# The first stage of a diffusion block in another order: x first on its queue, one-column token sums, projection from the first channels

## The chip, the core and the metric

One NeuronCore of a Trainium2 chip runs the whole program; the other seven are unused. The time is the device time of one execution in microseconds (us). Five engines work beside each other and meet only at semaphores: TensorE (PE; its weight loads have a row of their own, PEld), VectorE (DVE), ScalarE (ACT), GpSimd (POOL) and SyncE (SP), which here only issues transfers. Each engine takes its instructions in the order in which they stand on it.

## The reference

One layer of a transformer-like block on 512 tokens of 1024 channels, with 256 context tokens. What matters here is how it begins:

```
c_act = silu(c);  cc_act = silu(c_ctx)
shift, scale = parts of (c_act @ w_mod + b_mod)        # one value per channel
h = rmsnorm(x, norm1_g) * (1 + scale) + shift          # rmsnorm: x * rsqrt(mean over channels of x*x + eps) * g
proj = h @ w_in                                        # pooling, Fourier, Hyena, attention, gates
# Hyena's filters: two sine layers, a linear layer, a decay, a spectrum
f = sin(freq * (feats @ w1 + b1));  f = sin(freq * (f @ w2 + b2));  f = (f @ w3 + b3) * (decay + 0.05)
f = f / sum |f|
```

Behind that come the four branches, their gated merge, the output projection, a second norm, a gated feed-forward network with 2816 hidden channels and a last norm.

## The kernel before, in words

Channels lie on the partitions, in eight tiles of 128; the 512 tokens lie along the free dimension. A product in nearly full float32 precision is made of three passes: each operand is split into a high part (rounded to the type fp32r) and a low rest, and `mm3` (line 99) adds high x high, high x low and low x high. ACT makes the high part of a weight tile (tile `winh`), DVE the low one (`winl`); the same is done to the normalized x (`hxh`, `hxl`).

The change is in the first stage, lines 211 to 491. Between lines 387 and 491 the flag `pinned` is set, so that each engine's instructions keep exactly the order in which the calls stand there; behind it a scheduler orders the work. The stage has four threads:

- Statistics of x. `square(k)` (line 267) squares channel tile k on ACT, and PE multiplies the square by a matrix of ones (tile `pss`), which sums over the channels. `stat_sums` copies one row and turns it so that tokens lie on the partitions (`pst`). `rms_cols` (line 142) makes 1/sqrt on DVE and ACT from it, `rms_rows` (line 157) spreads that over the partitions with four diagonal matrices `dg` (PE, tile `pb`), and ACT copies it to `rb`.
- Modulation. `load_mod(kt)` loads 1 MB of weights (`wm`, four buffers), `mod(kt)` (line 348) multiplies them by c (PE, tile `pmod`; ACT copies it to `mrow`), and `mod_cols(kt)` (line 356) turns `mrow` to channels on the partitions (PE, tile `pmodt`; three small DVE operations `modk`, `acol`).
- The norm of tile kt: `norm` (DVE `hm`, ACT `hxh`) and `norm_low` (DVE `hxl`); then `estep(kt)` (line 382) adds this channel tile to three output tiles of the input projection (tile `pin`, three passes each).
- Hyena's filters: `sine_in`, `sine_arg`, `sine_out` for two layers (PE `pf`, ACT `san`, DVE `san`, ACT `h`), `fw3_fold` (DVE), `filt(s)` for four quarters of the taps (PE `ph`, DVE `khat`, ACT `vx`), `filt_abs`, and `fold(0..5)` (PE `pKe`, `pKo`).

Before, the threads are interleaved by twos: `mod` of two tiles, other PE work, then `mod_cols` of both, then the norm of both, and `estep` later. All loads stand on SP: first five small tables, then x, then weights.

Of the kernel before, what the change touches and what calls it, by code (L numbers as in the profile page):

```python
# [8 lines left out]
F32 = mybir.dt.float32  # L9
# [37 lines left out]
def block_kernel(ctx: ExitStack, tc: tile.TileContext, A):  # L47
# [3 lines left out]
    # an engine whose instructions keep the program's order while pinned is set  # L51
# [104 lines left out]
    # the same, spread over the partitions (tokens on the free dimension)  # L156
# [9 lines left out]
    # the table of the square root, loaded ahead of its use  # L166
# [18 lines left out]
    with ExitStack() as mix:  # L185
# [22 lines left out]
        # =================== start: modulation, first norm, filters of hyena ===================  # L208
# [6 lines left out]
        with ExitStack() as st:  # L215
# [19 lines left out]
            # filters of hyena: the two sine layers  # L235
            sines = (("h1", fw1, feats, h1), ("h2", fw2, h1, h2[0:64]))
            sans = []

            def sine_in(layer):
                _, w, src, _ = sines[layer]  # L240
                sans.append(yslot("san", (64, 4, TC), F32))
                for h, c in enumerate(halves):
                    p = ps("pf")[0:64, :TC]
                    PE.matmul(p, w, src[:, c], start=True, stop=True)
                    S.activation(sans[layer][:, h], p, AF.Identity, bias=frb[:, layer:layer + 1], scale=fr[:, 0:1])

            def sine_arg(layer):
                an = [(sans[layer][:, h], sans[layer][:, 2 + h]) for h in range(2)]
                for a, n in an:
                    V.tensor_scalar(n, a, INV2PI, MAGIC, ALU.mult, ALU.add)  # L250
                for a, n in an:
                    V.tensor_scalar(n, n, -MAGIC, None, ALU.add)
                for c in (C1, C2, C3):
                    for a, n in an:
                        V.scalar_tensor_tensor(a, n, -c, a, ALU.mult, ALU.add)
                for a, n in an:
                    V.tensor_scalar(a, a, PI_LO, -PI_LO, ALU.min, ALU.max)

            def sine_out(layer):
                dst = sines[layer][3]  # L260
                for h, c in enumerate(halves):
                    S.activation(dst[:, c], sans[layer][:, h], AF.Sin)
# [25 lines left out]
            # the sum of both directions' magnitudes is the larger magnitude of their sum and difference  # L288
# [24 lines left out]
            # transform at the odd frequencies f < 128; from sums over t = 4 u + r for each r follow those of  # L313
            # f, 511 - f, 255 - f and 256 + f (the second and third with the sine part negated)
            def fold(j):
# [11 lines left out]
                else:  # L327
                    # tabK's last part is that of t mod 4 = 3 negated
# [12 lines left out]
            # shift and scale of the first norm, channel tile by channel tile, for c and c_ctx  # L341
# [40 lines left out]
            def estep(kt):  # L382
                for m in range(NE):
# [4 lines left out]
            preload_sqrt(ones[:, 0:1])  # L388
            Y.dma_start(cols, A["cols"])
            V.tensor_scalar(frb, fr[:, 1:3], fr[:, 0:1], None, ALU.mult)  # L390
            Y.dma_start(feats, A["feats"])
            Y.dma_start(fw1, A["fw1"])
            Y.dma_start(fw2, A["fw2"])
            Y.dma_start(cc, A["cc"])
# [6 lines left out]
            Y.dma_start(sel, A["sel"])  # L401
            sine_arg(0)
            Y.dma_start(ident, A["ident"])
            load_mod(0)
            square(2)
            load_early()
            square(3)
            sine_out(0)
            fw3_fold()
            square(4)  # L410
            square(5)
            S.activation(cc, cc, AF.Silu)
            sine_in(1)
            load_mod(1)
            sine_arg(1)
            square(6)
            square(7)
            split_early()
            sums = stat_sums()
            rcx = rms_cols(sums)  # L420
            Y.dma_start(dec, A["dec"])
            load_mod(2)
            sine_out(1)
            mod(0)
            mod(1)
            load_mod(3)
            S.copy(rbx, rms_rows(rcx))
            mod_cols(0)
            mod_cols(1)
            norm(0)  # L430
            norm(1)
            filt(0)
            filt(1)
            norm_low(0)
            filt_abs(0)
            load_early()
            norm_low(1)
            split_early()
            load_early()
            mod(2)  # L440
            load_mod(4)
            split_early()
            load_mod(5)
            mod(3)
            filt(2)
            estep(0)
            estep(1)
            filt_abs(1)
            mod_cols(2)
            Y.dma_start(tabK, A["tabK"])  # L450
            mod_cols(3)
            norm(2)
            mod(4)
            mod(5)
            load_mod(6)
            norm(3)
            norm_low(2)
            fold(0)
            load_mod(7)
            fold_sum(0)  # L460
            filt(3)
            mod_cols(4)
            mod_cols(5)
            norm(4)
            norm_low(3)
            norm(5)
            mod(6)
            norm_low(4)
            fold(1)
            estep(2)  # L470
            estep(3)
            mod_cols(6)
            mod(7)
            norm(6)
            norm_low(5)
            fold_sum(1)
            norm_low(6)
            estep(4)
            mod_cols(7)
            norm(7)  # L480
            estep(5)
            filt_abs(2)
            fold(2)
            estep(6)
            norm_low(7)
# [3 lines left out]
            filt_abs(3)  # L489
# [27 lines left out]
        # =================== input projection, hyena ===================  # L517
# [694 lines left out]
```

## Time and profile before

| | us |
|---|---|
| median of 3 runs (range) | 866.44 (866.24 to 866.78) |
| span of the profiled execution | 864.0 |
| the median run, less that span | 2.4 |
| PE busy in the span | 843.5 (98%) |
| DVE, ACT, POOL busy | 501.2, 333.1, 6.0 |
| start of the first `pmod` in the stage | 20.83 |
| end of the stage's last filter product (`pKe`) | 68.47 |

The profile gives no time of its own for the profiled execution beyond its span; what lies around the span is taken to be the 2.4 us by which the median run is longer. A busy PE is not a PE at its peak, since matmuls overlap; so the table is no proof of a bound, and the rows below are.

### The profile page before, as it was taken

The page shows a single profiled execution, that of the slowest core. Times are in us where ns is not written, and L with a number is a line of the kernel's source. Part 1 is how long each engine was busy: PE and PEld are TensorE (multiplying, and loading weights), DVE is VectorE, ACT ScalarE, POOL GpSimd, SP SyncE. Part 2 cuts the span into 40 slices and gives each one's busy share as a digit, 9 for nine tenths or more (in the row PEclk, how much of TensorE's full clock was granted, in tenths as well). Part 3 has the DMA queues.
Part 4 walks back from the last instruction along what each step waited for, and adds up shares of the span by engine and source line. Part 5 has one row for each costly group of instructions (what it writes and reads, how often), then busy time and mean ns, then how long its engine had stood idle before and what let it go on. Part 6 is the DMA issues. An engine that isn't in the chain of part 4 may idle for free.

```text
span 864.0 us, 10732 instructions
## 1 busy us (share of the span) xinstructions
PE 843.5 (98%) x4192; PEld 685.5 (79%) x4192; DVE 501.2 (58%) x870; ACT 333.1 (39%) x519; POOL 6.0 (1%) x16
## 2 busy tenths in 40 slices
PE   6999999989999999999999999999999999999996
PEld 2577889777777778888888998888888888888886
DVE  4879997698797773444444774444444444233233
ACT  7544452625453342323333363333333333232321
POOL 0100000000000000000000000000000000000000
PEclk9999999999999999999999999999999999999998
DMA  8912214545555532223332222222222223223222
GB/s 315 414 50 74 98 43 162 164 168 180 195 183 183 199 137 92 91 92 116 124 126 98 73 89 108 98 98 98 98 98 98 98 94 95 86 92 91 86 68 98
DMA packets 30362, 107.30 MB, mean 124 GB/s; under 512 B 3783, under 2 KB 4935, under 8 KB 29288
## 3 DMA queue, kind: packets, MB, share of 16 engines
q1 hardware_dynamic: 30312, 106.62, 35.2%
q8 instruction: 33, 0.54, 0.2%
q14 instruction: 17, 0.14, 0.0%
HBM read 104.51 MB, written 2.10 MB: 123 GB/s over the span
## 4 chain that ended last, share of the span: by engine, by line
PE 86%; DVE 8%; ACT 2%; DMA 2%; issue 1%; SPq 0%; DVEq 0%; ACTq 0%
PE pup L60 28%; PE pin L60 25%; PE pdn L60 14%; PE pwo L60 5%; PE pbr L60 5%; PE psc L60 1%; DVE za L60 1%; PE pav L60 1%; PE pKe L60 1%; PE psl L60 1%; DVE winl L60 1%; DVE zb L60 1%; PE ptl L60 1%; DMA cb<-in_crow_dram 1%; PE pmod L60 1%
## 5 line engine op out<-in xcount | busy, mean ns | idle before, releaser
L60 PE MATMUL pup<-hxh,wupl 128*128 128x512 f32 (+1 forms) x376 | 140.8, 376 | 0.0
L60 PE MATMUL pup<-hxl,wuph 128*128 128x512 f32 (+1 forms) x376 | 140.6, 376 | 0.0
L60 PE MATMUL pup<-hxh,wuph 128*128 128x512 f32 (+1 forms) x376 | 139.9, 376 | 0.7 <-ACT wuph L60 0.4
L60 PE MATMUL pdn<-act,wdnh 128*128 128x512 f32 (+1 forms) x396 | 112.7, 368 | 0.0
L60 PE MATMUL pin<-hxh,wgh 128*128 128x512 f32 x256 | 101.4, 396 | 0.6 <-ACT wgh L60 0.6
L60 PE MATMUL pin<-hxh,wgl 128*128 128x512 f32 x256 | 100.5, 393 | 0.0
L60 PE MATMUL pin<-hxl,wgh 128*128 128x512 f32 x256 | 100.3, 392 | 0.0
L60 DVE TENSOR_TENSOR wupl<-wupr,wuph 128x1024 fp32r<-128x1024 f32 x44 | 53.9, 1225 | 71.5 <-ACT wuph L60 69.7
L60 ACT CAST wuph<-wupr 128x1024 fp32r<-128x1024 f32 x44 | 46.3, 1053 | 92.3 <-PE pup L60 86.3
L60 PEld LDWEIGHTS pdn<-act,wdnh 128*128 128x128 f32 x396 | 71.6, 189 | 12.0
L60 PEld LDWEIGHTS pup<-hxh,wuph 128*128 128x128 f32 x376 | 70.1, 188 | 13.8 <-ACT wuph L60 0.6
L60 PEld LDWEIGHTS pup<-hxh,wupl 128*128 128x128 f32 x376 | 70.7, 188 | 12.9 <-DVE wupl L60 0.2
L60 PEld LDWEIGHTS pup<-hxl,wuph 128*128 128x128 f32 x376 | 70.6, 188 | 12.9
L60 PE MATMUL pdn<-act,wdnl 128*128 128x512 f32 (+1 forms) x198 | 72.4, 366 | 0.0
L60 ACT ACTIVATE sg<-pin 128x512 f32<-128x512 f32 x32 | 19.2, 600 | 119.5 <-PE pin L60 119.5
L60 DVE TENSOR_TENSOR wdnl<-wdnr,wdnh 128x1024 fp32r<-128x1024 f32 (+1 forms) x24 | 27.2, 1134 | 63.2 <-ACT wdnh L60 63.1
L60 DVE SCALAR_TENSOR_TENSOR sg<-sg,pbr 128x512 f32<-128x512 f32 x24 | 16.5, 688 | 80.2 <-PE pbr L60 80.2
L60 PEld LDWEIGHTS pin<-hxh,wgh 128*128 128x128 f32 x256 | 48.1, 188 | 10.8 <-ACT wgh L60 1.0
L60 PEld LDWEIGHTS pin<-hxh,wgl 128*128 128x128 f32 x256 | 48.1, 188 | 10.5 <-issue 0.5
L60 PEld LDWEIGHTS pin<-hxl,wgh 128*128 128x128 f32 x256 | 48.1, 188 | 10.1 <-issue 0.5
L60 PE MATMUL pin<-hxh,winh 128*128 128x512 f32 x128 | 51.7, 404 | 0.0
L60 ACT CAST wdnh<-wdnr 128x1024 fp32r<-128x1024 f32 (+1 forms) x24 | 23.6, 982 | 72.4 <-PE pdn L60 66.7
(265 smaller groups left out, 1429.2 us busy)
## 6 DMA issues: line engine op xcount, KB each, us to landing
wupr<-in_wup_dram SPq DMA_DIRECT2D x44, 512.0 KB, 3.4
wgr<-in_wg_dram SPq DMA_DIRECT2D x32, 640.0 KB, 3.8
wm<-in_wmB_dram SPq DMA_DIRECT2D x32, 512.0 KB, 4.7
wm<-in_wmA_dram SPq DMA_DIRECT2D x8, 1024.0 KB, 10.7
winr<-in_win_dram SPq DMA_DIRECT2D x16, 512.0 KB, 3.5
wdnr<-in_wdn_dram SPq DMA_DIRECT2D x16, 512.0 KB, 3.4
wor<-in_wout_dram SPq DMA_DIRECT2D x8, 512.0 KB, 3.5
wdnr<-in_wdn_dram SPq DMA_DIRECT2D x8, 384.0 KB, 3.0
```

Source lines behind the costliest of these rows:

```text
L60: ins = f(*a, **k)
```

## The change

The order of the stage's calls is new, and some pieces are computed in another way:

- SP loads x first; the five small tables (`cols`, `feats`, `fw1`, `fw2`, `cc`) are issued by ACT. `ident` and `sel` follow x, and the weights follow in another order.
- `square` runs on DVE for tiles 0, 1, 2 and 7, on ACT for 3 to 6. Four products with a single column of ones, the square as the stationary operand, put the sums on the token partitions at once; `stat_sums` is gone.
- The tables of Silu and of the square root are loaded ahead of the statistics, the sine's table once, behind them.
- The sine layers' two token halves stand on 64 partitions each, so that `sine_arg` has 6 operations instead of 12. `fw3_fold` runs on POOL.
- Each channel tile goes through `mod`, `mod_cols`, `norm`, `norm_low` by itself, and the projection's `estep` of the tile before stands between them.

```diff
             def sine_in(layer):
                 _, w, src, _ = sines[layer]
-                sans.append(yslot("san", (64, 4, TC), F32))
-                for h, c in enumerate(halves):
+                sans.append(yslot("san", (P, 2, TC), F32))
+                for r, c in zip(rows, halves):
...
             def sine_arg(layer):
-                an = [(sans[layer][:, h], sans[layer][:, 2 + h]) for h in range(2)]
-                for a, n in an:
-                    V.tensor_scalar(n, a, INV2PI, MAGIC, ALU.mult, ALU.add)
...
+                a, n = sans[layer][:, 0], sans[layer][:, 1]
+                V.tensor_scalar(n, a, INV2PI, MAGIC, ALU.mult, ALU.add)
...
             def square(k):
                 sq = tmp(T)
-                S.activation(sq, xs[k], AF.Square)
-                PE.matmul(pss, ones, sq, start=k == 0, stop=k == KT - 1)
-
-            def stat_sums():
-                S.copy(ssq[0:1], pss[0:1])
-                pst = ps("pst")
+                if k in (0, 1, 2, 7):
+                    V.tensor_mul(sq, xs[k], xs[k])
+                else:
+                    S.activation(sq, xs[k], AF.Square)
                 for i in range(4):
-                    PE.matmul(pst[:, i:i + 1], ssq[0:1, i * P:(i + 1) * P], ones[0:1, 0:1], start=True, stop=True)
-                return pst[:, 0:4]
+                    PE.matmul(pss[:, i:i + 1], sq[:, i * P:(i + 1) * P], ones[:, 0:1], start=k == 0 and i == 0,
+                              stop=k == KT - 1, skip_group_check=True)
...
-                    V.tensor_tensor(fw3s[d].rearrange("p (o c) -> p o c", o=2), wv[:, :, 0], wv[:, :, 1], op)
+                    G.tensor_tensor(fw3s[d].rearrange("p (o c) -> p o c", o=2), wv[:, :, 0], wv[:, :, 1], op)
...
-            def estep(kt):
-                for m in range(NE):
+            def estep(kt, ms=range(NE)):
+                for m in ms:
```

The list of calls itself, up to the third channel tile (one or two calls a line here; the two lists, not a line diff):

```
before: preload_sqrt; cols; frb; feats, fw1, fw2, cc; x 0..7; fw3; sine_in(0); square(0), (1); sel; sine_arg(0);
  ident; load_mod(0); square(2); load_early; square(3); sine_out(0); fw3_fold; square(4), (5); Silu(cc); sine_in(1);
  load_mod(1); sine_arg(1); square(6), (7); split_early; stat_sums; rms_cols; dec; load_mod(2); sine_out(1);
  mod(0), mod(1); load_mod(3); rms_rows, rb; mod_cols(0), (1); norm(0), (1); filt(0), (1); norm_low(0); filt_abs(0);
  load_early; norm_low(1); split_early; load_early; mod(2); load_mod(4); split_early; load_mod(5); mod(3); filt(2);
  estep(0), (1); filt_abs(1); mod_cols(2); tabK; mod_cols(3); norm(2); mod(4), mod(5); ...
after: ACT: cols, feats, fw1, fw2, cc. SP: x 0..7; ident; sel; load_mod(0); load_early; load_mod(1); fw3; load_early;
  load_mod(2); dec; load_mod(3). frb; Silu(cc); preload_sqrt; sine_in(0); square(0) .. (3); sine_arg(0); square(4) .. (7);
  rms_cols; rms_rows, rb; mod(0); sine_out(0); sine_in(1); split_early; mod_cols(0); norm(0); norm_low(0); sine_arg(1);
  sine_out(1); fw3_fold; mod(1); split_early; load_early; tabK; load_mod(4); mod_cols(1); norm(1); norm_low(1);
  estep(0, first two); filt(0); mod(2); load_mod(5); split_early; mod_cols(2); norm(2); norm_low(2); estep(1, first two);
  estep(0, third), estep(1, third); filt(1); filt_abs(0); mod(3); load_mod(6); mod_cols(3); norm(3); norm_low(3);
  estep(2); filt(2); filt_abs(1); mod(4); load_mod(7); mod_cols(4); ...
```

How this stands on PE, from the statistics to the projection's first passes: before,

```order
L60 MATMUL pst<-ones,ssq 128x1 x4
L60 MATMUL pmod<-wm,cc 32x256 x16
L60 MATMUL pb<-dg,ones 128x128 x4
L60 MATMUL pmodt<-sel,mrow 128x2 x4
L60 MATMUL ph<-fw3d,h_109 128x512 x4
L60 MATMUL pmod<-wm,cc 32x256 x16
L60 MATMUL ph<-fw3d,h_109 128x512 x2
L60 MATMUL pin<-hxh,winh 128x512
```

and of the changed kernel:

```order
L60 MATMUL pss<-ones,hm 128x1 x32
L60 MATMUL pb<-dg,ones 128x128 x4
L60 MATMUL pmod<-wm,cc 32x256 x8
L60 MATMUL pf<-h_109,fpk 64x256 x2
L60 MATMUL pmodt<-sel,mrow 128x2 x2
L60 MATMUL pmod<-wm,cc 32x256 x8
L60 MATMUL pmodt<-sel,mrow 128x2 x2
L60 MATMUL pin<-hxh,winh 128x512
```

Between a `pmod` and the `pmodt` that needs its copy there was other PE work for two tiles (`pb`, or `ph` and `pin`); now the two stand next to each other, and the second sine layer's `pf` stands ahead of the first `pmodt`. The four filter products `ph` that stood ahead of the first `pin` now stand behind it.

On ACT, from the square root on: before,

```order
L60 ACTIVATE rr<-rv 128x4
L60 ACT_TABLE_LOAD
L60 ACTIVATE h_109<-san 64x256 x2
L60 COPY mrow<-pmod 128x256 x2
L60 COPY rb<-pb 128x512
L60 ACTIVATE hxh<-hm,modk 128x512 x2
```

and of the changed kernel:

```order
L60 COPY rb<-pb 128x512
L60 COPY mrow<-pmod 128x256
L60 ACT_TABLE_LOAD
L60 ACTIVATE h_109<-san 64x256 x2
L60 ACTIVATE san<-pf,frb,cols 64x256 x2
L60 CAST winh<-winr 128x1024
L60 ACTIVATE hxh<-hm,modk 128x512
L60 ACTIVATE h_109<-san 64x256 x2
L60 COPY mrow<-pmod 128x256
L60 CAST winh<-winr 128x1024
```

The copies `mrow` of the first two tiles stood side by side. Now the first sine layer's end, the second sine layer, a weight tile's cast and the first tile's `hxh` stand between them.

On DVE, over the same stretch of the changed kernel (before, both layers' `san` operations stood ahead of the statistics' `rv`):

```order
L60 TENSOR_SCALAR dg<-ident,rr 128x128 x4
L60 TENSOR_TENSOR winl<-winr,winh 128x1024
L60 TENSOR_SCALAR modk<-pmodt,cols 128x2 x2
L60 TENSOR_SCALAR acol<-modk,cols 128x2
L60 SCALAR_TENSOR_TENSOR hm<-xt,acol,rb 128x512
L60 SCALAR_TENSOR_TENSOR hxl<-hm,modk,hxh 128x512
L60 TENSOR_SCALAR san<-san 128x256 x2
L60 SCALAR_TENSOR_TENSOR san<-san 128x256 x3
L60 TENSOR_SCALAR san<-san 128x256
L60 TENSOR_TENSOR winl<-winr,winh 128x1024
```

The second sine layer's six operations moved from ahead of the statistics to behind the first tile's norm. From the stage's end on, the order on PE, DVE and ACT is the same in both kernels.

## Rows read from the trace of the kernel before

**Rows 1.** Chain of waits, 0 to 75 us: start, us, what ran.
```profile
20.83 1.86 PE pmod L60 x32
...
43.52 0.79 PE pmodt L60 x8
...
47.23 4.12 PE pin L60 x18
...
63.32 5.15 PE pKe L60 x12
68.47 0.79 PE psn L60 x8
```
**Rows 2.** Busy time by stretch: engines' us, granted clock, DMA share, GB/s.
```profile
46.00:69.00 23.00, 23.00 (x104) 15.64 (x103) 16.77 (x30) 11.83 (x19) 0.29 (x4) 1.00 0.07 28
```
**Rows 3.** Instructions in time, SP and ACT: start, us, engine, operation, [idle before].
```profile
3.22 3.75 SPq L60 DMA_DIRECT2D xt<-in_xT_dram  x8
6.21 0.63 ACT L60 ACTIVATE hm<-xt 128x512 f32<-128x512 f32 x1 [0.23 <-DMA xt<-in_xT_dram]
```
**Rows 4.** Busy time by stretch, while x lands.
```profile
7.00:9.00 2.00, 2.00 (x3) 0.97 (x4) 2.00 (x8) 1.26 (x2) 0.00 (x0) 1.00 0.96 292
```
**Rows 5.** Instructions in time, PE's weight loads for the squares.
```profile
10.53 0.34 PEld L60 LDWEIGHTS pss<-hm,ones 128*128 128x128 f32 x1 [0.52 <-issue]
...
18.10 0.19 PEld L60 LDWEIGHTS pss<-hm,ones 128*128 128x128 f32 x1 [0.24 <-issue]
```
**Rows 6.** Instructions in time, PE: one-column sums of the last norm.
```profile
847.20 0.36 PE L60 MATMUL pst<-ones,ssq 128*128 128x1 f32 x2
847.42 0.36 PE L60 MATMUL pst<-ones,hm 128*128 128x1 f32 x2
```
**Rows 7.** Busy time by stretch, the end of the program.
```profile
856.00:858.00 2.00, 0.97 (x8) 0.78 (x8) 0.78 (x5) 0.20 (x1) 0.00 (x0) 0.99 0.00 0
858.00:860.00 2.00, 0.00 (x0) 0.00 (x0) 1.67 (x6) 1.01 (x2) 0.00 (x0) 0.50 0.04 14
```
**Rows 8.** Instructions in time, ACT, 14 to 25 us.
```profile
15.55 1.01 ACT L60 ACTIVATE san<-pf,frb,cols 64x256 f32<-64x256 f32 x2 [0.40 <-PE pf L60]
...
17.83 1.05 ACT L60 CAST winh<-winr 128x1024 fp32r<-128x1024 f32 x1 [0.23 <-DMA winr<-in_win_dram]
...
21.29 1.28 ACT L60 ACT_TABLE_LOAD   x1
22.59 0.72 ACT L60 ACTIVATE h<-san 64x256 f32<-64x256 f32 x2
23.21 0.62 ACT L60 COPY mrow<-pmod 128x256 f32<-128x256 f32 x2
24.27 0.59 ACT L60 COPY rb<-pb 128x512 f32<-128x512 f32 x1 [0.44 <-PE pb L60]
```
**Rows 9.** Instructions in time, DVE, 19 to 26 us.
```profile
19.63 1.21 DVE L60 TENSOR_TENSOR winl<-winr,winh 128x1024 fp32r<-128x1024 f32 x1
20.87 0.16 DVE L60 TENSOR_SCALAR rv<-pst 128x4 f32<-128x4 f32 x1
```
**Rows 10.** Instructions in time, DVE and ACT, one channel tile's norm.
```profile
51.73 0.35 DVE L60 TENSOR_SCALAR modk<-pmodt,cols 128x2 f32<-128x2 f32 x2 [3.66 <-PE pmodt L60]
...
52.38 0.75 DVE L60 SCALAR_TENSOR_TENSOR hm<-xt,acol,rb 128x512 f32<-128x512 f32 x1
53.16 0.72 ACT L60 ACTIVATE hxh<-hm,modk 128x512 fp32r<-128x512 f32 x1
```
**Rows 11.** Tile san: ns min/median/max, first and last start, form.
```profile
L60 DVE SCALAR_TENSOR_TENSOR san<-san x12: 409/409/411, 6.6 to 18.9; 64x256 f32<-64x256 f32 x12
```
**Rows 12.** Instructions in time, DVE and ACT, one quarter of the filters.
```profile
43.12 1.28 DVE L60 TENSOR_TENSOR khat<-ph,dec 128x512 f32<-128x512 f32 x2
43.84 1.23 ACT L60 ACTIVATE vx<-khat 128x512 f32<-128x512 f32 x2 [2.05 <-DVE khat L60]
```
**Rows 13.** Tile khat, POOL's part: ns min/median/max, first and last start.
```profile
L60 POOL TENSOR_SCALAR khat<-khat x1: 1814/1814/1814, 29.8 to 29.8; 1x512 f32<-1x512 f32 x1
```

More of the change, by code (lines that the diff above doesn't have):

```diff
@@ L387, in block_kernel @@
             pinned[0] = True
[L388 to L394, printed above, removed]
+            S.dma_start(cols, A["cols"])
+            S.dma_start(feats, A["feats"])
+            S.dma_start(fw1, A["fw1"])
+            S.dma_start(fw2, A["fw2"])
+            S.dma_start(cc, A["cc"])
             for k in range(KT):
                 Y.dma_start(xs[k], A["xT"][:, k])
-            Y.dma_start(fw3, A["fw3"])
+            Y.dma_start(ident, A["ident"])
+            Y.dma_start(sel, A["sel"])
+            load_mod(0)
+            load_early()
+            load_mod(1)
+            Y.dma_start(fw3, A["fw3"])
+            load_early()
+            load_mod(2)
+            Y.dma_start(dec, A["dec"])
+            load_mod(3)
+            V.tensor_scalar(frb, fr[:, 1:3], fr[:, 0:1], None, ALU.mult)
+            S.activation(cc, cc, AF.Silu)
+            preload_sqrt(ones[:, 0:1])
             sine_in(0)
@@ L400, in block_kernel @@
             square(1)
-            Y.dma_start(sel, A["sel"])
+            square(2)
+            square(3)
             sine_arg(0)
[L403 to L409, printed above, removed]
             square(4)
             square(5)
[L412 to L415, printed above, removed]
             square(6)
@@ L417, in block_kernel @@
             square(7)
+            rcx = rms_cols(pss[:, 0:4])
+            pb = rms_rows(rcx)
+            S.copy(rbx, pb)
+            mod(0)
+            sine_out(0)
+            sine_in(1)
             split_early()
[L419 to L422, printed above, removed]
+            mod_cols(0)
+            norm(0)
+            norm_low(0)
+            sine_arg(1)
             sine_out(1)
-            mod(0)
+            fw3_fold()
@@ L425, in block_kernel @@
             mod(1)
[L426 to L437, printed above, removed]
             split_early()
             load_early()
+            Y.dma_start(tabK, A["tabK"])
+            load_mod(4)
+            mod_cols(1)
+            norm(1)
+            norm_low(1)
@@ L440, in block_kernel @@
+            estep(0, range(2))
+            filt(0)
             mod(2)
-            load_mod(4)
+            load_mod(5)
             split_early()
-            load_mod(5)
-            mod(3)
+            mod_cols(2)
+            norm(2)
+            norm_low(2)
+            estep(1, range(2))
+            estep(0, range(2, 3))
+            estep(1, range(2, 3))
+            filt(1)
+            filt_abs(0)
+            mod(3)
+            load_mod(6)
+            mod_cols(3)
+            norm(3)
@@ L445, in block_kernel @@
+            norm_low(3)
+            estep(2)
             filt(2)
-            estep(0)
-            estep(1)
             filt_abs(1)
[L449 to L452, printed above, removed]
             mod(4)
+            load_mod(7)
+            mod_cols(4)
+            norm(4)
+            norm_low(4)
+            estep(3)
+            filt(3)
+            filt_abs(2)
             mod(5)
-            load_mod(6)
-            norm(3)
@@ L457, in block_kernel @@
-            norm_low(2)
+            mod_cols(5)
+            norm(5)
+            norm_low(5)
             fold(0)
-            load_mod(7)
+            estep(4)
             fold_sum(0)
[L461 to L466, printed above, removed]
+            filt_abs(3)
             mod(6)
-            norm_low(4)
+            mod_cols(6)
+            norm(6)
+            norm_low(6)
             fold(1)
-            estep(2)
@@ L471, in block_kernel @@
-            estep(3)
-            mod_cols(6)
+            estep(5)
+            fold_sum(1)
             mod(7)
[L474 to L478, printed above, removed]
             mod_cols(7)
             norm(7)
-            estep(5)
-            filt_abs(2)
+            norm_low(7)
+            estep(6)
             fold(2)
-            estep(6)
-            norm_low(7)
             estep(7)
@@ L488, in block_kernel @@
             fold(4)
-            filt_abs(3)
             fold(5)
```

16 lines of the change are left out of this document (7 added, 9 removed).

## The prediction

> **What bounds the kernel now.** I read the chain of waits first, then busy time by stretch, then the instructions of the first 70 us. The chain runs through PE from the first modulation product at 20.83 us to the last filter product, which ends at 68.47 when `psn` begins [rows 1]; from 46 to 69 us PE has no idle time at all [rows 2]. So the stage is a start (0 to 20.83, PE waiting on the statistics) and a PE-bound rest. Behind 68.47 the order of work is the same in both kernels and PE stays the bound, so I carry the shift of that point to the end, one for one. Is the rest really PE's own work? Prices from [rows 1]: a tile's `pmod` 0.93 (1.86 for two), its `pmodt` 0.39 (0.79 for two), a 512-column float32 product 0.86 (six `pKe` in 5.15; I use it for `ph` too), a `pin` pass 0.229 (18 in 4.12). The stage holds 8 x 0.93 + 8 x 0.39 + 8 `ph` and 12 fold products x 0.86 + 72 x 0.229 = 7.4 + 3.1 + 17.2 + 16.5 = 44.2 us; from 20.83 to 68.47 are 47.6 us. With 1.4 for `pb`, waiting takes only some 2 us. The old interleaving by twos hides nearly every copy.
>
> The sum is made against the profiled execution: span 864.0 and 2.4 around it, which is the median of the runs shown, 866.4, by construction.
>
> **What the change removes.** The statistics' tail of `ssq` copy and `pst`, about 1.6 us; two of five ACT table loads; six of twelve operations of each sine layer on DVE. x is issued at 0.74 instead of 3.22 [rows 3]. That doesn't move its last tile by 2.5 us: x0 is used 3.0 us after its issue [rows 3], and x moves at 292 GB/s with the DMA engines busy 0.96 of the time [rows 4], so 2.1 MB of x and 0.3 MB of tables take 8.2 us whoever issues them. From a start of the bytes near 2.5 us the last tile lands at about 11 (bounds 9.5 and 12.5). [...]
>
> **The new path at full PE rate.** The last square on DVE 0.7 (like a `khat` product, 0.64 each for two in 1.28 [rows 12]), then four one-column products at 0.21 [rows 6], with a little queueing behind the tiles ahead: sums at 13.0. From `rv` (20.87 [rows 9]) to the end of the `rb` copy (24.27 + 0.59 [rows 8]) took 4.0, so `rb` is at 17.0, and `mrow` of tile 0 at 17.7. Before, `rb` was at 24.86: a lead of almost 8 us. Now what stands, in order, between this and PE's `pmodt` of tile 1: ACT holds that tile's `mrow` behind `sine_out(1)`, DVE holds `sine_arg(1)` behind tile 0's norm, and that norm stands behind the cast's low part. One chain:
>
> sine table 1.28 and `sine_out(0)` 0.72 [rows 8]; `pf` and `san` of layer 1, 1.6 (the pair of `san` alone 1.01); the weight cast 1.05; `winl` 1.21 [rows 9]; `modk`, `acol` 0.65 (51.73 to 52.38), `hm` 0.75, `hxh` 0.72 [rows 10]; `hxl` 0.75, taken like `hm`; `sine_arg(1)`: three two-input operations of 0.41 [rows 11] and three lighter ones of about 0.28, with 0.04 between them, 2.3; `sine_out(1)` 0.72; `mrow` 0.31 (two in 0.62). The sum is 12.1, with a dozen hand-overs of some 0.03 about 12.4: `pmodt` of tile 1 starts at 30.1. PE has done two `pmod`, one `pmodt` and `pf` by then and idles for nearly 8 us. What is queued behind that `pmodt` on PE is the whole rest of the stage.
>
> Work left: 44.2 - 2 x 0.93 - 0.39 = 41.9, so 72.0 without further waits. Each tile now adds one, as `pmodt` follows its own `pmod` at once. For tiles 4 and 5: from the first `ph`'s end the second `khat` ends 1.55 later, its `vx` at 2.2, the queued `mrow` at 2.6 [rows 12, 8], while `pmod` ended at 0.86 + 0.93 = 1.8: 0.9 us of waiting each. Tiles 6 and 7 have no filter ahead of the copy: 0.5 each. For tiles 2 and 3 the casts of the second and third weight tile (1.05 on ACT and 1.21 on DVE) stand in the same queue: 1.1 for the low part of the second weight tile, 2.4 before `pmodt` of tile 2, 1.7 for tile 3. Together 8.0: the stage ends at 80.0, against 68.47. **At full rate the kernel is 11.5 us slower: 877.9.**
>
> **PE's rate in the start** is the cost that these rows only bound. [...] At the program's end it fell to 0.50 at 858, right after two microseconds in which PE was busy for 0.97 with transposes and one-column products [rows 7]. The changed start has only such thin work: one-column sums, short products, then 8 us of nothing. Lower bound: the one-column products do raise the clock, 0. Upper: nothing before the projection does. Then a one-column product costs 0.21 x 0.34/0.19 = 0.38, a tile 1.5, and eight tiles behind two slow `pf` end at 18.4 instead of 13.0: 5.4. `pb`, `pmod`, `pf` at half rate add 3.0 on the chain, and `pmodt` of tile 1 is at 38.5. The first 4 to 5 us of dense work at half rate cost 2.3, but they cover the waits of tile 2, so that nothing is added. Together 8.5. I take the upper one, since the row nearest to this work [rows 7] shows the clock falling beside it: 877.9 + 8.5 = 886.4.
>
> [...]
>
> **Costed at nothing.** `fw3_fold` on POOL: a 512-column operation there took 1.8 us [rows 13] on one partition; two are 3.6, from about 19 us when `fw3` is in; `ph` needs it past 32, and without that cover it would cost the rest. Squares on DVE and the first sine layer: beside x's landing. The five issues on ACT, some 2.5 us as on SP before (0.74 to 3.22): ahead of anything that ACT could do. Silu and the square-root table: beside x's landing; on ACT's path the tables cost 2.6 us before 7.5. Weight loads: SP issues the last `wm` behind context tiles that wait for tile 2's norm, at about 44; it is used past 67, so some 18 us of cover.
>
> **Rivals.**
> A, the clock rises during the sums: 877.9, or 880 with the dense work after the gap alone at half rate. [...] Against: [rows 7].
> B, the lead decides (the other side). The price of a late `rb` is gone, PE starts its `pmod` at 16.4 instead of 20.83, and the copies are ready when PE comes for them: 866.4 - 4.4 = 862. It decides if `mrow` of tile 1 is there by about 22, which the ACT order shown does not allow unless the sine layer's chain of 12 us shrinks below 5. Small.
> C, x doesn't land earlier at all: at full rate x at 12.5 adds 1.5, 879.4; at half rate PE is behind x anyway and nothing changes.
> D, the clock stays low or falls again between the tiles' waits: each 5 us of dense work more at half rate costs 2.3 to 2.5, so 889 to 892.
>
> **How the numbers follow.** Forecast, half rate until the projection: 0.50 (own range 883 to 890). A with C: 0.33 (875 to 882). D: 0.10. B: 0.05. Something that cancels: 0.02. Two medians of this kernel closer than about 0.2% (1.7 us) can't be told apart. Faster is B, 0.05; within 0.2% 0.03; slower 0.92. The range leaves out B and part of the ends: 875 to 891.
>
> **What would show it.** In the profile after: the last x tile used by about 11 to 12; weight loads of `pss` 0.1 or 0.2 us apart (rate); `rb` at 17 or 23; a PE gap of 6 to 8 us ahead of the second tile's `pmodt`, put down to ACT's `mrow`; gaps of 0.5 to 2.4 us ahead of each later one; `psn` at 80 to 88 instead of 68.47. The prediction is wrong if that gap is under 3 us, or if the work behind 68.47 takes up the shift.

## The result, and the profile after

The changed kernel is slower: 889.48 us (median of 4 runs, 888.68 to 890.09) against 866.34 beside it (4 runs), a ratio of 1.027 with a 95% interval of 1.0255 to 1.0284. The forecast was 886.4, the range 875 to 891. The span grew from 864.0 to 887.7; the 23.1 us in the median are that, less 0.6 around the span.

The page's first part shows that PE's busy time grew by 11.0 us (843.5 us before), the span by 23.7; the rest is waiting:

```profile
PE 854.5 (96%) x4232; PEld 697.6 (79%) x4232; DVE 501.4 (56%) x860; ACT 328.8 (37%) x512; POOL 8.0 (1%) x18
```

The chain of waits (start, us, what), against [rows 1]:

```profile
1.83 4.08 DMA fpk<-in_fw_dram
...
7.98 13.76 PE pss L60 x64
...
23.54 2.40 PE pb L60 x8
...
41.24 1.01 PE pmodt L60 x4
42.25 2.77 PE pin L60 x6
...
92.94 0.79 PE psn L60 x8
```

`psn`, the first product behind the stage, moved from 68.47 to 92.94: 24.5 us, of which 0.8 come back by the end of the span. The one-column sums take 13.76 us and end at 21.7, later than the 512-column sums of before, whose last two tiles end at 19.1:

```profile
17.14 2.00 PE pss L60 x4
```

So x's early issue gives `rb` no lead: its copy starts at 25.97, at 24.27 before [rows 8].

Then PE waits for the second tile's `mrow`. PE's waits from 23 to 42 us, then from 42 to 95 (what waited for what: us in all, times, longest):

```profile
PE pmodt L60 <- ACT mrow L60: 6.5, 1, 6.5
...
PE pmodt L60 <- ACT mrow L60: 4.3, 6, 1.0
```

What ACT and DVE do in that time, both in one list (start, us, engine, operation, idle time before it):

```profile
27.87 0.37 ACT L60 COPY mrow<-pmod 128x256 f32<-128x256 f32 x1 [1.31 <-PE pmod L60]
28.25 1.28 ACT L60 ACT_TABLE_LOAD   x1
29.54 0.85 ACT L60 ACTIVATE h<-san 64x256 f32<-64x256 f32 x2
...
32.59 1.05 ACT L60 CAST winh<-winr 128x1024 fp32r<-128x1024 f32 x1
33.67 1.23 DVE L60 TENSOR_TENSOR winl<-winr,winh 128x1024 fp32r<-128x1024 f32 x1 [8.59 <-ACT winh L60]
...
35.45 0.75 DVE L60 SCALAR_TENSOR_TENSOR hm<-xt,acol,rb 128x512 f32<-128x512 f32 x1
36.24 0.72 ACT L60 ACTIVATE hxh<-hm,modk 128x512 fp32r<-128x512 f32 x1 [2.60 <-DVE hm L60]
...
38.31 1.34 DVE L60 SCALAR_TENSOR_TENSOR san<-san 128x256 f32<-128x256 f32 x3
...
40.08 0.85 ACT L60 ACTIVATE h<-san 64x256 f32<-64x256 f32 x2 [3.12 <-DVE san L60]
40.84 0.35 ACT L60 COPY mrow<-pmod 128x256 f32<-128x256 f32 x1
```

Read it as one chain: where no dots stand between two lines, the second starts within 0.2 us of the end of the one it needs, on the other engine or the same; behind the dots are the second layer's `pf` and `san`, the tile's `modk` and `acol`, `hxl`, and the other `san` operations. The wait is for work that has nothing to do with the second tile's `mrow` but stands ahead of it on ACT.

The busy time in four stretches (PE, PEld, DVE, ACT, POOL; clock; DMA share; GB/s):

```profile
8.00:21.70 13.70, 13.70 (x64) 13.63 (x64) 2.85 (x7) 4.00 (x8) 2.49 (x2) 1.00 1.02 397
21.70:41.20 19.50, 9.05 (x49) 4.71 (x48) 7.33 (x22) 7.25 (x13) 0.00 (x0) 1.00 0.55 217
41.20:47.00 5.80, 5.76 (x13) 4.00 (x14) 3.44 (x7) 1.77 (x2) 0.00 (x0) 1.00 0.90 334
47.00:92.90 45.90, 41.63 (x226) 24.21 (x225) 31.75 (x59) 20.18 (x34) 3.63 (x7) 1.00 0.26 88
```

The clock is printed as 1.00 all along, but the first projection passes start 0.43 apart and later ones 0.23:

```profile
42.69 0.63 PE L60 MATMUL pin<-hxl,winh 128*128 128x512 f32 x1
43.11 0.63 PE L60 MATMUL pin<-hxh,winl 128*128 128x512 f32 x1
...
57.39 0.39 PE L60 MATMUL pin<-hxl,winh 128*128 128x512 f32 x1
57.62 0.40 PE L60 MATMUL pin<-hxh,winl 128*128 128x512 f32 x1
```

So until near 47 us PE ran at about half of its later rate (half rate, or the lower level, below); the four records of filter products (`ph`) that stand there from 44.82 take 2.86 us, the next four, from 52.72, 1.88.

### The profile page after: what moved, and what is told of

Same layout as the page of the kernel before. It is cut to its first block, busy times and chain, and to the rows that moved or that the text cites. A ratio compares the mean times of both kernels' runs of the same rounds, so it can differ in the third digit from the quotient of the medians.

```text
span 887.7 us, 10802 instructions
## 1 busy us (share of the span) xinstructions
PE 854.5 (96%) x4232; PEld 697.6 (79%) x4232; DVE 501.4 (56%) x860; ACT 328.8 (37%) x512; POOL 8.0 (1%) x18
## 3 DMA queue, kind: packets, MB, share of 16 engines
q1 hardware_dynamic: 29856, 106.30, 36.3%
## 4 chain that ended last, share of the span: by engine, by line
PE 86%; DVE 8%; ACT 3%; DMA 1%; issue 1%; ACTq 0%; DVEq 0%; SPq 0%
PE pup L60 27%; PE pin L60 24%; PE pdn L60 14%; PE pwo L60 5%; PE pbr L60 5%; PE pss L60 2%; PE psc L60 1%; DVE za L60 1%; PE pav L60 1%; PE pKe L60 1%; PE psl L60 1%; DVE winl L60 1%; DVE zb L60 1%; PE ph L60 1%; PE ptl L60 1%
## 5 line engine op out<-in xcount | busy, mean ns | idle before, releaser
L60 PE MATMUL pin<-hxh,winl 128*128 128x512 f32 x128 | 50.8, 397 | 0.0
```

Source lines behind the costliest of these rows:

```text
L60: ins = f(*a, **k)
```

## The experiments

All times stand beside runs of the kernel before on the same chip (866.49, 866.23, 865.93 and 866.17 for the four groups). "Stage end" is where `psn` starts: 68.47 before, 92.94 in the changed kernel.

**One-column sums alone, in the kernel before.**

```diff
-                PE.matmul(pss, ones, sq, start=k == 0, stop=k == KT - 1)
+                for i in range(4):
+                    PE.matmul(pss[:, i:i + 1], sq[:, i * P:(i + 1) * P], ones[:, 0:1], ...)
...
-            sums = stat_sums()
+            sums = pss[:, 0:4]
```

> The kernel before with one part of the change alone: the token sums are made by 32 one-column products, straight into the columns that the norm reads (the copy of one row to SBUF and the four small products behind the squares are gone); x, the tables and the channel order stay as they were. My theory: it is the one-column work that keeps TensorE's clock low. Before, the clock record rises at 11.7 us, while the 512-column products of the squares run; here it should stay at half until the tiles' first 512-column products, later by 5 us or more, and the small first products and the first tiles at half rate cost more than the 1.6 us saved at the sums' end: 868 to 872 us. Rival: the low clock in the changed kernel comes from the empty stretches behind the sums and not from the products' shape; then the clock rises here as before and the shorter tail shows: 864.5 to 866.5 us.

870.15 us, ratio 1.0044 (1.0029 to 1.0059), as my theory had it. The chain of waits:

```profile
24.22 3.57 PE pmod L60 x32
27.79 0.57 PE pb L60 x2
```

Two tiles' `pmod` take 3.57 instead of 1.86 [rows 1]: PE is still at half rate up to 27.8 us. In the kernel before, the squares' weight loads stand 0.86 apart at 10.5 us [rows 5] and 0.43, full rate, from about 12 us on. The sums' shape alone costs 3.7 us, net of the shorter tail behind them.

**512-column sums in the changed kernel.**

```diff
-                for i in range(4):
-                    PE.matmul(pss[:, i:i + 1], sq[:, i * P:(i + 1) * P], ones[:, 0:1], ...)
+                PE.matmul(pss, ones, sq, start=k == 0, stop=k == KT - 1)
...
-            rcx = rms_cols(pss[:, 0:4])
+            rcx = rms_cols(stat_sums())
```

> The changed kernel with one part undone: the squares go through 512-column products again, with the copy of one row and four small products behind them; x first, the tables' places and the channel order stay. My theory: about half of the 23.7 us lost is the clock and the price of the one-column products, half the new order. Then the clock record rises near 12 us, the sums are through at 15 to 17 us instead of 21.7, the stage's last narrow product starts near 83 us instead of 92.9, and the time is 878 to 882 us. Rival 1 (the order alone costs it all, the shape nothing): 888 to 891 us. Rival 2 (the shape of the sums alone costs it all): 864 to 868 us.

887.52 us, 1.0245 (1.0229 to 1.026): 2 us back instead of 9. My size was wrong, and rival 1 was nearly right. The sums did end at 17.4, but two things ate the lead. First, DVE and POOL (instructions in time):

```profile
19.57 0.18 DVE L60 RECIPROCAL rr<-rr 128x4 f32<-128x4 f32 x1 [0.27 <-ACT rr L60]
19.78 0.75 DVE L60 TENSOR_TENSOR rt<-rr 128x4 f32<-128x4 f32 x1
20.57 1.18 DVE L60 TENSOR_TENSOR rt<-rt,rv 128x4 f32<-128x4 f32 x1
21.78 0.17 DVE L60 TENSOR_SCALAR rt<-rt 128x4 f32<-128x4 f32 x1
```

Two operations on four columns take 0.75 and 1.18 instead of 0.16, 1.6 us more in all, while `fw3_fold` runs on POOL from 19.25 to 21.73; each ends within 0.05 us of one of POOL's two operations. In the changed kernel POOL is done 0.06 us before this chain begins. Second, the clock (same columns as above):

```profile
27.00:29.00 2.00, 0.33 (x2) 0.19 (x2) 0.00 (x0) 1.97 (x3) 0.00 (x0) 1.00 0.02 6
30.00:42.50 12.50, 6.02 (x30) 4.18 (x31) 7.49 (x17) 4.39 (x7) 0.00 (x0) 0.50 0.68 263
```

It fell at 22.7, after PE had stood from 19.1 to 22.5, rose at 26.1 and fell again at 29.5, after a stop from 26.5 to 28.7, until 43.2. So with 512-column sums too the clock is low behind the new order's gaps.

**Added products, to raise the clock.**

```diff
+            busy(4, start=True)
             sine_in(0)
             square(0)
+            busy(1, 2)                  # and behind squares 1 to 6
...
+            busy(2)
             pb = rms_rows(rcx)
...
+            busy(3)
             sine_in(1)
...
+            busy(10)
             mod_cols(1)
```

> The changed kernel with products added whose result nobody reads: ones times ones into unused columns of the sums' bank, four of 384 columns ahead of the first sine layer, one of 256 columns behind the products of each of the first seven squares, two ahead of the products that spread the norm, three ahead of the second sine layer and ten ahead of the second tile's small products. They add about 10 us of TensorE work at full rate in stretches in which it mostly waits. My theory: the low clock, kept low by one-column work and by waiting, is what costs about half of the loss; with these products the clock record rises before 20 us, the second tile's projection starts near 34 us instead of 41.2 and runs at full rate (2.8 us a tile instead of 5.8), and the time falls to 879 to 884 us though TensorE has more to do. Rival: the clock follows something else (time since the start, or the load of the engines together), it rises at 47 us as before, and the added work makes it 890 to 897 us.

893.56 us, 1.0304 (1.0281 to 1.0327): my theory fell, the rival's number held, but not its reason. PE by stretch, and then its products from 6.5 to 10.3 us and the one-column ones from 12 to 24 (shape, records | us, mean ns of one):

```profile
6.50:10.50 4.00, 4.00 (x24) 3.19 (x25) 1.24 (x3) 3.54 (x7) 0.00 (x0) 1.00 0.99 324
11.00:25.00 14.00, 13.97 (x56) 12.98 (x56) 1.84 (x4) 1.29 (x3) 2.49 (x2) 0.50 1.01 414
31.50:44.30 12.80, 11.54 (x54) 6.09 (x50) 5.28 (x12) 6.46 (x11) 0.00 (x0) 1.00 0.41 157
```

```profile
L60 PE MATMUL pss<-ones,hm 128*128 128x1 f32 x16 | 2.0, 246 | 0.0
L60 PE MATMUL pf<-fpk 33*64 33x256 f32 x4 | 1.4, 492 | 0.0
L60 PE MATMUL pss<-ones 128*128 128x256 f32 x3 | 1.1, 434 | 0.0
...
L60 PE MATMUL pss<-ones,hm 128*128 128x1 f32 x38 | 8.2, 334 | 0.0
```

The clock rose while the first `pf` ran, near 7.2 us (it took 1.38 instead of 1.94), and fell at 10.6 although PE was busy without a break, about half of the time with one-column products. It was low until 31, so that the added work itself ran at half rate and held the sums up to 25. From 31.1 on the clock was full, and yet the second tile's `pmodt` began at 44.35, which is 12.3 us after the first tile's `mrow` (end 32.08). That chain belongs to ACT and DVE: PE at full rate shortens it by only 0.7 us.

**The modulation's rows one tile ahead.**

```diff
             mod(0)
+            mod(1)
             sine_out(0)
...
-            mod(1)
+            mod(2)
...
-            mod(2)
+            mod(3)                      # and so on
```

> The changed kernel with the row products of each tile's modulation (mod, with its copy on ScalarE) issued one tile ahead, where those of the tile before stood; the rest of the order is untouched. My theory: the short gaps ahead of each tile's small products (.5 to 1.0 us in tiles 2 to 7, 4.3 us in all) and a part of the 6.5 us gap of the second tile are the wait of a product for the copy of a row that was made right before it; ahead, these gaps go to zero for tiles 2 to 7 and the second tile still waits for its weights: 883 to 886 us. Rival: the same time is waited elsewhere (TensorE then waits for the shifted and scaled channels instead, which come no earlier): 888 to 890 us, with the gaps now in front of the projections.

885.07 us, 1.0218 (1.0202 to 1.0233): 4.4 less, as my theory had it, and the stage end went to 87.75. The rival was right on the place of the first wait. PE in time:

```profile
36.93 0.53 PE L60 MATMUL pin<-hxh,winh 128*128 128x512 f32 x1 [3.11 <-ACT hxh L60]
...
42.22 0.80 PE L60 MATMUL pin<-hxh,winh 128*128 128x512 f32 x1 [3.29 <-ACT winh L60]
```

The 6.5 us are now 6.4 in front of the projection, in two parts, at the same point of the chain. What was gained are the six later waits (4.3 us).

**The second sine layer ahead of the norm**, added to that.

```diff
             sine_arg(0)
+            sine_out(0)
             square(4)
             square(5)
+            sine_in(1)
             square(6)
+            split_early()
+            sine_arg(1)
             square(7)
+            sine_out(1)
+            preload_sqrt(ones[:, 0:1])
             rcx = rms_cols(pss[:, 0:4])
...
-            sine_out(0)
-            sine_in(1)
-            split_early()
...
-            sine_arg(1)
-            sine_out(1)
```

> The changed kernel with the rows of the modulation one tile ahead (as in the run before) and the second sine layer, its table and the first early weights' split moved into the 7 us in which ScalarE and VectorE wait for the sums; the square root's table is loaded once more behind them, and the sums stay one-column products. My theory: the second tile's small products waited for one chain on ScalarE and VectorE (sine table, second sine layer, weight split, first tile's norm); with the sine layer out of it they start near 31 us instead of 41.8, TensorE has no gap over 3 us left between them and the norm, and the time is 874 to 878 us. Rival: that gap is set by what is loaded then (third early weights and the fifth tile's rows are asked for at 35 us) or by TensorE's clock, so the same stretch is waited a few instructions later: 882 to 885 us.

881.64 us, 1.0179 (1.0164 to 1.0194): 3.4 less, under half of what I expected, and 0.4 below the rival's range. I had put the layer where it holds up the sums (PE in time):

```profile
21.90 1.87 PE L60 MATMUL pss<-ones,hm 128*128 128x1 f32 x8 [1.31 <-ACT hm L60]
26.93 1.86 PE L60 MATMUL pss<-ones,hm 128*128 128x1 f32 x8 [3.17 <-DVE hm L60]
```

`rb` slid to 33.06; the wait moved to the other side of the norm. So this run doesn't tell the price of the chain.

**The same with 512-column sums.** The edit is that of the second experiment.

> The same with the sums as 512-column products again (and the copy of a row and four small products behind them). My theory: the sums end near 17.5 instead of 22.5 us; since the sine layer must still fit beside them on ScalarE, 2 to 4 us of that reach the end: 871 to 875 us, and 2 to 4 us below the run with one-column sums. Rival: the sums were not the late ones any more, the second sine layer was: no difference between the two, within 1 us.

883.57 us, 1.0201 (1.0185 to 1.0216), 1.9 more: both expectations missed. The last square waits 5.8 us behind the sine layer, and the clock is at 0.50 from 21 to 38 us:

```profile
26.24 2.07 PE L60 MATMUL pss<-hm,ones 128*128 128x512 f32 x2 [5.80 <-DVE hm L60]
```

`fw3_fold` meets DVE's work here as well. POOL is busy from 19.94 to 23.40, and beside it two DVE operations (by their place `winl` and the first `san`) fill 20.23 to 23.00, 2.77 us; in the changed kernel, with POOL idle, they take 1.23 (33.67) and 0.31 (37.66).

**x first alone, in the kernel before.**

```diff
-            Y.dma_start(cols, A["cols"])   # and feats, fw1, fw2, cc
+            S.dma_start(cols, A["cols"])   # and feats, fw1, fw2, cc
...
-            sine_in(0)
             square(0)
             square(1)
+            sine_in(0)
```

> The kernel before with x first alone: the five small tables go out on ScalarE's queue, x is the first on SyncE's, and the first two squares stand ahead of the first sine layer in the program. All squares stay on ScalarE, the sums stay 512-column products, the order behind stays. My theory: x's last tile lands 2 to 2.5 us earlier, but ScalarE's squares of tiles 6 and 7 stand behind the sine layers, the Silu and their table loads, and these wait for tables that now land later; the sums end within 1 us of before: 865 to 868 us. Rival: the lead passes through to the end: 862.5 to 864.5 us.

869.62 us, 1.0037 (1.0024 to 1.005): no lead, as I thought, but 1.6 us more loss than my range allowed. The first `pf` now starts at 9.22, behind two squares' products at half rate (3.75 us for four records from 5.54 on, 1.98 from 20.99 on); it started at 3.45 before:

```profile
9.22 1.97 PE L60 MATMUL pf<-fpk 33*64 33x256 f32 x4
```

In addition, ACT's last two squares stand behind both sine layers' parts, and with them they move from 16.46 to 20.31.

**Two other starts.** The first has x first, five squares on VectorE, all squares ahead of the second sine layer, five added products at the start and the order of before behind the norm.

> The kernel before in its own order behind the norm, with the parts of the change that looked useful ahead of it: x first, small tables on ScalarE's queue, five squares of eight on VectorE, both sine layers on all 128 partitions, Silu first; and with all squares ahead of the second sine layer, 512-column sums, and five products of ones times ones at the start whose result nobody reads, to have TensorE at full rate by 6 us. My theory: the sums end near 13.5 us instead of 19.2, the norm's row is spread at 19 to 21 instead of 24.9, and 3 to 5 us of that reach the end of the stage, since TensorE has work without gaps behind it: 861 to 864 us. Rival: the stage behind is bound by the landings of the modulation's weights (the transfers are busy without a break from 6 to 46 us), so the lead is waited back: 865 to 867 us.

871.1 us, 1.0057 (1.004 to 1.0073): theory and rival both missed. `rb` came at 25.66, behind the second tile's row, and the clock was low from 18.6 to 25.4 and from 28.8 to 32.2. The next one mended both, with added products in its waits for the clock:

```diff
             pb = rms_rows(rcx)
-            split_early()
+            S.copy(rbx, pb)
+            sine_arg(1)
             mod(1)
...
             filt(1)
+            split_early()
```

> The kernel before in its own order behind the norm and a start in a third order: x first with the small tables on ScalarE's queue, Silu as ScalarE's first work, five squares on VectorE and three on ScalarE all ahead of the second sine layer, 512-column sums, the square root's table loaded beside the sums' small products, the norm's row copied ahead of the second tile's row, and nine products of ones times ones whose result nobody reads (four at the start, one in each of three waits, two ahead of the filters) so that TensorE's clock stays up. My theory: the earlier try lost its lead because rows of the second tile stood ahead of the norm's row on ScalarE and the clock was low from 18.8 to 32 us; without both, the sums end near 14 us, the norm's row is there near 20 us instead of 24.9, and the stage ends 3 to 5 us earlier: 861 to 864 us. Rival: TensorE's work behind is held by the landings of weights, so nothing of the lead remains: 865 to 868 us.

870.73 us, 1.0059 (1.0043 to 1.0076): theory and rival missed again. `rb` started at 21.52, 2.8 us early, but I had moved the first weight split behind the filters, and the third weight tile takes the buffer of the first, so it is asked for only when the first is split, at 32.52 us. Its landing in the chain of waits:

```profile
32.52 3.64 DMA winr<-in_win_dram
```

**The halves apart.** First the start of before with the tile-by-tile order of the changed kernel (`...` stands for it), the second sine layer and first split ahead of the norm:

```diff
             rcx = rms_cols(sums)
             Y.dma_start(dec, A["dec"])
+            load_early()
             load_mod(2)
+            load_mod(3)
             sine_out(1)
-            mod(0)
-            mod(1)
+            pb = rms_rows(rcx)
+            S.copy(rbx, pb)
+            mod(0)
+            mod_cols(0)
+            norm(0)
...
```

> The first part of the kernel before (its loads, its 512-column sums, its early sine layers and first weight split) joined to the changed kernel's order from the spread norm on, tile by tile: rows, shift and scale, normalised channels, projection of that tile, then the next tile. It tells the price of the tile-by-tile order from that of the start. My theory: with the second sine layer and the first split done ahead of the norm, the first tile's chain (row copy, small products, shift and scale, three passes over the tile: about 4 us) is all that stands before the second tile's small products; they start near 29 us instead of 41.2, the later tiles wait for their rows as in the changed kernel (4 to 5 us in all), the stage's last narrow product starts near 77 us: 873 to 876 us, so that some 8 of the 23.7 us belong to the tile-by-tile order and 15 to the start. Rival 1: the tile-by-tile order costs nothing by itself, all is the start: 866 to 868 us. Rival 2: it costs nearly all: 884 us or more.

879.56 us, 1.016 (1.0145 to 1.0175): 13.6 over before, between my theory and rival 2. The chain of waits:

```profile
19.57 1.05 ACT winh L60
...
24.01 2.40 PE pb L60 x8
...
32.38 1.01 PE pmodt L60 x4
```

Without the sine layer and the first split the second tile's `pmodt` comes 3.7 us after the first `mrow`'s end (28.71), not 13.0. It is later than I said because x's fourth tile was used 0.9 us later in this run (10.65, 9.72 before), because the cast ahead of the sums' copy waited for its weight tile (19.57; 17.83 before [rows 8]), and because the clock fell at 22.6 and stayed low until 36.3. The waits for `mrow` are 5.5 us in all, 8 times; the six of the later tiles are 4.3, as in the changed kernel.

Then the counterpart: the start of the changed kernel, with the order of before behind it.

```diff
             S.copy(rbx, pb)
             mod(0)
+            mod(1)
             sine_out(0)
             sine_in(1)
             split_early()
             mod_cols(0)
-            norm(0)
-            norm_low(0)
+            mod_cols(1)
             sine_arg(1)
             sine_out(1)
             fw3_fold()
+            norm(0)
+            norm(1)
+            filt(0)
...
```

> The changed kernel's first part up to the norm's row (x first, small tables on ScalarE's queue, one-column sums, the square root's table early), joined to the order of the kernel before: both first tiles' rows, shift and scale together, filters, then two tiles at a time; the second sine layer stands behind the norm as in the changed kernel. The counterpart of the run that joined the other halves (879.6 us, 13.6 above before). My theory: the norm's row comes at 26 us as in the changed kernel, no lead over the 24.9 of before; the filters wait for the second sine layer until about 36 us (24.9 before) and find TensorE at its low clock, while the rows of two tiles and the sums fill 2 to 3 us of it: 876 to 880 us, so that each half alone costs 10 to 14 us and the two overlap by 2 to 4. Rival 1: the start costs only what its late sums cost, 869 to 872 us. Rival 2: the start is most of it, 883 us or more.

881.81 us, 1.018 (1.0166 to 1.0194): 15.6 over before, 2 more than I said. PE in time:

```profile
40.02 5.24 PE L60 MATMUL ph<-fw3d,h 128*128 128x512 f32 x8 [5.20 <-ACT h L60]
```

and in the kernel before:

```profile
24.88 3.68 PE L60 MATMUL ph<-fw3d,h 128*128 128x512 f32 x8
```

The filters wait for the second sine layer until 40.02 and take 5.24 instead of 3.68, the first of them at half rate (the clock is at 0.50 until 43.2). So either half alone costs 14 to 16 us, and the whole 23: they overlap by 6. What both traces have in common is a low clock (0.50 from 22.6 to 36.3 us in the one, from 33.0 to 43.2 in the other) and PE waiting for rows or layers that are late on ACT. That these two are the overlap is read from the traces and not tested by itself.

**The start that paid**, with the first split back ahead of the norm's row:

```diff
+            split_hi()                  # cast of the first early weights, ACT
             pb = rms_rows(rcx)
             S.copy(rbx, pb)
             sine_arg(1)
+            split_lo()                  # their low part, DVE
             mod(1)
```

> The try before with three edits: the first early weights are split ahead of the norm's row (their cast on ScalarE before the row is copied, their difference on VectorE before the second tile's products), so that the third early weights are asked for 10 us earlier; the products that spread the norm no longer stand behind the first tile's rows and an added product; three squares of x go through ahead of the first sine layer. Five squares on VectorE, three on ScalarE; added products whose result nobody reads: three at the start, one beside the copy of the sums, one ahead of the filters. My theory: the norm's row is there near 19.5 to 20.5 us (24.9 before, 22.1 in the last try), the filters start near 22.8 us (24.9 before), since the second sine layer is then the late one, and TensorE has no gap behind it: 863 to 865 us, 1 to 3 below before. Rival: something late stands behind this lead too (the landings of weights, VectorE's share of the splits), and the end of the stage stays: 866 to 869 us.

864.59 us (11 runs), 0.9983 (0.9974 to 0.9992): 1.6 us below the kernel before, as my theory had it. That is no more than the 1.7 us that the prediction called hard to tell apart, but over 11 and 15 runs the interval stays below 1. ACT's copy, PE's filters and the stage end:

```profile
19.92 0.59 ACT L60 COPY rb<-pb 128x512 f32<-128x512 f32 x1 [0.18 <-PE pb L60]
```

```profile
23.46 3.67 PE L60 MATMUL ph<-fw3d,h 128*128 128x512 f32 x8 [0.60 <-issue]
```

```profile
66.66 0.79 PE psn L60 x8
```

`rb` leads by 4.3 us, the filters by 1.4, the stage end by 1.8. The rest of the lead stops at the second sine layer, whose `h` begins at 22.95, no earlier than before (22.59 [rows 8]). Behind the filters the chain of waits runs through the landing of the third weight tile (22.73 to 30.47), but PE waits only about 0.1 us for its low part.

## Why the prediction was right, and where its sizes were off

- **The chain on ACT and DVE: right.** It was put at 12.4 us from the first `mrow`'s end to the second tile's `pmodt`. It took 13.0 (28.24 to 41.24), and 12.3 with PE at full rate, in the run with added products. The gap on PE was 6.5 us, put down to `mrow`, in the 6 to 8 forecast. Taking the second sine layer and the first split out of it brought it to 3.7 us.
- **The clock: right.** Half rate until the projection, with no rise during the sums (their products stand 0.43 apart to 21.7 us), so A falls. D falls too: the clock was full from about 47 us on (a tile's `pmod` 1.93 at 32.84, 1.07 at 47.61). The sum takes half rate to last for 4 to 5 us of dense work behind the gap. That was an estimate, and no run shows it there: the squares' loads of the kernel before stood 0.85 apart from 7.97 to 11.38 us, and here the work behind the gap was at half rate for 5.8 us (41.2 to 47.0). The term of 8.5 us was not bought back by changing the sums alone (2.0 us): in that run the clock fell again behind the gaps, to 0.50 at 22.7 and at 29.5, and two DVE operations took 1.6 us more beside POOL's work; neither had I said. C can't be told: the last square waits for PE's sums (16.70, after 4.83 us of waiting), not for x.
- **The sums: mis-sized.** They were to end at 18.4 at half rate and ended at 21.7. A one-column product took 0.43, not 0.38 (64 records in 13.76 us), which is 1.8 us: I scaled 0.21 by how long the weight loads take (0.34 and 0.19), while their distances, 0.86 and 0.43 in the same [rows 5], give a factor of 2. And the sums began at 7.98, some 1.6 later than assumed, as the tables' `fpk` landed 4.1 us after its issue (in the kernel before it was issued from 1.65 on and used at 3.45). For these reasons `rb`, with 23 named for the half rate, came 3 us later. B needed a lead of `rb`, and none came.
- **The rest of the stage: 51.7 us from the second tile's `pmodt` on, 50.0 forecast.** The later waits are 4.3 us, not 8.0: tiles 4 to 7 waited 2.6 us, 2.8 forecast, but tiles 2 and 3 only 1.7 instead of 5.2. Against that the half rate made the first 5.8 us of PE's work some 2.9 us longer. This is the cover that the prediction spoke of: the slow work fills the waits of tile 2. What the sum missed are small products done by themselves: a tile's `pmodt` takes 0.61 where I had halved 0.79 [rows 1], its `pmod` 1.04 and not 0.93, together 2.3 us in seven tiles.
- **The shift carried one for one: nearly.** Of 24.5 us 0.8 came back, and 0.6 around the span. 20.0 forecast and 23.1 measured differ by +2.7 at the second `pmodt` (sums 3.3 late, the way from there 0.6 shorter), +1.7 (the rest) and -1.4. That the total misses by only 3.1 us is in part luck: the 1.4 us that came back hide half of the 2.7.
- **Costed at nothing: `fw3_fold` on POOL, by luck.** It cost nothing only because the late sums let it end 0.06 us ahead of the norm's chain; with sums that end at 17.4 it cost 1.6 us.
- **Not settled**: what the changed order would cost at full rate throughout, since no run kept the clock up beside one-column sums; and how much of the first half's 15.6 us is the second sine layer's place. One-column sums and x first cost 3.7 and 3.4 alone, but the second of these has a price of its own in where the sine layer was put. The runs that moved the sine layer ahead of the norm in the changed order held up the sums with it.

## What to carry to other kernels

The wait named "for a copy" (6.5 us) was a wait for all that stood ahead of that copy in its engine's order: list that before moving anything in front of it, and keep two tiles in flight where a product needs a copy of the product before it (one tile ahead gave 4.4 us here). An early transfer pays only as far as the next late thing lets it: in the start that paid, 4.3 us of lead became 1.8. Fewer columns were no less work for TensorE here, where each product loads new weights (13.76 us for eight tiles at half rate, 1.7 a tile, as with 512 columns), and PE stayed at half rate to 27.8 us behind them (two tiles' `pmod` in 3.57 us, 1.86 before).

## What the runs showed of the hardware

- The clock fell to 0.50 at 10.6 us in the run with added products although PE was busy for 4.00 of 4.00 us ahead of it (6.50 to 10.50).
- A float32 one-column product with a new 128x128 weight (two records) takes 0.43 us at the lower level (64 records in 13.76 us) and 0.22 at the upper one (847.20 to 847.42 [rows 6]), about half. Four of them, one tile's sums, take 1.7 us at the lower level, as much as the tile's 512-column product (two records, 0.86 each [rows 5]).
- In the changed kernel the profile prints a clock of 1.00 up to 47 us too, where the projection's passes stand 0.43 apart (42.69 to 43.11), and 0.23 later (57.39 to 57.62); so the level was read there from the distance of equal products.
- In the changed kernel with 512-column sums two four-column DVE operations took 0.75 and 1.18 us beside POOL's two operations (19.25 to 21.73); the second ended 0.02 us behind them. In the changed kernel, with POOL done at 21.70, the same two took 0.16 each (22.40 and 22.60). The reciprocal, with a single tensor input, took its usual 0.18 at 19.57, in the middle of POOL's first.
